# The feed-forward down projection of a hybrid decoder trunk: where its row sums are split, who adds the fourth product's weights, and where the normalisation is emitted

## The chip, the cores and the metric

The kernel runs on one core of one Trainium2 chip. The metric is the device time of one launch in microseconds, the median of several runs; lower is better. The profile comes from one more execution on the same kind of chip, recorded by the hardware profiler. Engines are named as in the profile: PE is TensorE's matmul stream and PEld its weight loads, DVE is VectorE, ACT is ScalarE, POOL is GpSimd, SP is SyncE, which issues transfers.

## The reference

Two layers of a decoder trunk on 512 tokens of 1024 features in float32. Each layer has a feed-forward block, a mixer (a gated linear recurrence and a sliding-window attention side by side), and a second feed-forward block. The change touches the feed-forward blocks, of which the program has four:

```python
def rms_norm(x, gain):
    y = x * rsqrt(mean(x * x, axis=-1, keepdims=True) + EPS)
    return y * gain

def swiglu(h, w_gate, w_up, w_down):          # w_down: 2816 x 1024
    return (silu(h @ w_gate) * (h @ w_up)) @ w_down

for l in range(2):
    x = x + 0.5 * rms_norm(swiglu(rms_norm(x, g0), ...), g1)      # feed-forward 1
    x = x + rms_norm(mixed(rms_norm(x, g2)) @ w_out, g3)          # mixer
    x = x + 0.5 * rms_norm(swiglu(rms_norm(x, g4), ...), g5)      # feed-forward 2
```

## The kernel before, in words

**Precision.** Every float32 product is made of three matmuls in a reduced format: each operand is split into a high part (`hi`, a rounding copy made by ScalarE) and a low part (`lo`, what the copy left over). `lo` is made in one of two ways. `split` lets VectorE subtract (line 426 for activations, line 293 for weights of the quarter products, line 356 for other weights). `split_dma` lets ScalarE write the negated source and GpSimd issue an accumulating transfer that adds the copy's source to it (lines 435 to 437). `mm3` then issues hi x hi, hi x lo and lo x hi.

**The stage.** `down` (line 685) multiplies the activations (22 tiles of 128 features, `src`) by the weights of the down projection. Tokens come in four tiles `t` of 128, outputs in two halves `h` of 512, so there are eight accumulators `y[t][h]`. The features 16 to 21 are multiplied directly (`both`, `piece`): three weight blocks for `h` = 0 first, three for `h` = 1 at the end. The features 0 to 15 go through a Strassen-like scheme of seven products on quarters (`quarters`, line 878): features in two halves, tokens in two halves, outputs in two halves. Each product is 4 weight blocks ("quarters" `q` = 0 to 3 below), each used for 2 feature tiles x 2 token tiles x 3 matmuls of 512 columns, 48 matmuls in all. The order is p1, p3, p7, p2, p6, p5, then the second output half of token tiles 0 and 1, then p4, then the second output half of token tiles 2 and 3.

**Operands.** `Late` makes the left operands: `x1` for p1, `x37` for p3 and p7, `x56` from the row sums `s` for p5 and p6 (`more(k)`, by `split_dma`), `x2[0]` and `x2[1]` from the raw tiles for p2 and p4 (`second`, by `split_dma`). `Stream.quarter` (line 254) makes the right operands, one block per call: raw blocks `u` (for p1 and p7) and `v` (for p2) are loaded by SyncE into four buffers, and sums of quarters live in `b22` (p3, p5) and `b12` (p7, p6, p4). When a raw block is no longer needed, `leave` frees its buffer and issues the next load. A block is split up to four blocks ahead of the one in use; six pairs of `hi` and `lo` exist.

**What is emitted beside the products.** The functions `side1` to `side5` are called at each quarter `q` of their product, and emit work for other engines: row sums, splits, loads, and `fetch`, which loads the gain row and the eight pieces of the residual `x_d` (line 724). `ready(n)` splits the activations 16 to `n`-1 for the second output half.

**The end of the stage.** `half(t, h)` adds the pieces of a result, squares and sums it (line 624) and multiplies it by the gain. `post(t)` finishes the norm and adds the residual (line 831). Then `norm(t)` computes the next sub-layer's pre-norm (line 842), or, in the last feed-forward block of the program, `leave(t)` transposes and stores the output. `pre.turn(0, ...)` transposes token tiles 0 and 1 into the next stage's input after the last matmul of token tile 2, and `pre.turn(1, ...)` does tiles 2 and 3 a little later (line 124 for the transposes).

**What sets the order.** TensorE's instructions keep the order in which the program emits them; a modelled clock (`order.t`) decides where side work such as the transposes is interleaved. For the other engines a scheduler orders instructions by their place in the program and by when it thinks that their inputs are there; instructions given to `pin` keep the program's order among themselves. Engines execute their queues in order, so an instruction that waits holds up all that follow it in its queue.

Of the kernel before, what the change touches and what calls it, by code (L numbers as in the profile page):

```python
# [44 lines left out]
def trunk(ctx: ExitStack, tc: tile.TileContext, xin, wall, gains, lbT, hgain, sinks, c_dist, c_mask, c_ident, out):  # L45
# [109 lines left out]
    class Stream:  # L155
# [98 lines left out]
        def quarter(self, it):  # L254
# [3 lines left out]
            def sums(o, x, y, op):  # L258
                for c in range(2):
                    pin(nc.vector.tensor_tensor(o[c], x[c], y[c], op=op))  # L260

            def raw(i):
                self.load(i + 1)
                return [self.raw[i][:, c] for c in h]

            def leave(i):
                self.raw.pop(i)
                self.freed += 1
                self.load(self.freed + W32)
# [18 lines left out]
            if it.kind == "p7" and q + 1 < it.n:  # L288
                sums(self.b12[q + 1], self.b12[q + 1], self.b22[q + 1], ALU.add)
            elif it.kind == "p6":  # L290
                sums(self.b22[q], self.b22[q], w, ALU.add)
            for c in range(2):
                pin(nc.vector.tensor_tensor(it.lo[:, h[c]], w[c], it.hi[:, h[c]].bitcast(F32), op=ALU.subtract))  # L293
            if it.kind == "p7":

                sums(w, raw(u + q), w, ALU.subtract)
                leave(u + q)
            elif it.kind == "p6":
                for o, x in zip(w, raw(v + q)):
                    nc.gpsimd.dma_start(o, x, accum_op=ALU.add)  # L300
                leave(v + q)
            elif it.kind == "p5":
                self.b22[q] = None
            elif it.kind == "p4":
                self.b12[q] = None
# [379 lines left out]
    def down(src, kt, l, n, nxt, fast):  # L685
# [12 lines left out]
        def ready(n):  # L698

            for i in range(2 * js[0], min(n, kt)):  # L700
                if not isinstance(src[i], tuple):
                    src[i] = split(src[i])
# [31 lines left out]
        if fast:  # L734
# [32 lines left out]
            def side7(q):  # L767
                for k in (2 * q, 2 * q + 1):
                    late.second(0, k)

            def side2(q):
                for k in (2 * q, 2 * q + 1):
                    late.more(k)

            def side6(q):
                for k in (2 * q, 2 * q + 1):
                    late.second(1, k)

            def side5(q):
                if q == 1:  # L780
                    fetch()
                elif q > 1:
                    ready(2 * js[0] + 3 * q - 3)

            more, product = quarters(late, y, (side1, side3, side7, side2, side6, side5))
        else:
# [48 lines left out]
        def norm(t):  # L835
# [5 lines left out]
            for h in range(2):  # L841
                nc.vector.tensor_scalar(pre.xn[t][h], xt[t][h], rc, None, op0=ALU.mult)

        def rest():
            yield WAIT["normed"]
            pre.turn(1, lambda kp: acc() if kp == 0 else aux())
# [4 lines left out]
        bs = [ws.next(8, TT) for _ in last]  # L851
        for t in range(TT):
            if fast and t == 2:
                product(4, [y[t][0] for t in (2, 3)], False)
                for t in (2, 3):
                    half(t, 0)
                t = 2
            for j, b in zip(last, bs):
                for i in range(2):
                    piece(b, t, 1, j, i)  # L860
                    order.poll()
                ws.used(b)
                if pre and (t, j) == ((2, last[-1]) if fast else (3, last[TURN])):
                    pre.turn(0, lambda kp: acc() if kp < 3 else aux())
                    if not fast:
                        norm(2)
            post(t)
            if not pre:
                order.spawn(leave(t))
            elif fast or t != 2:  # L870
                norm(t)
        if pre:
            order.spawn(rest())
        else:
# [696 lines left out]
```

## Time and profile before

| | |
|---|---|
| time, three runs | 2159.26, 2160.92, 2160.66 us, median 2160.66 us |
| the profiled execution: own time, span | 2160.11 us, 2158.3 us |
| mean granted TensorE clock | 0.988 |
| PE busy | 2096.1 us (97%) |
| DVE busy | 1632.0 us (76%) |
| ACT busy | 1243.8 us (58%) |
| POOL busy | 285.1 us (13%) |
| transfers from and to memory | 213.43 MB read, 14.73 MB written |

The span runs from the first to the last instruction; the own time also counts what lies around them. Busy PE does not mean a PE at its peak: the ends of matmuls are modelled, so their start times tell more than their durations. In a group's row the columns are the line, the engine and operation, output and input names, count, busy time and mean duration, and the idle time in front with what ended it. In a row of windows the columns are the stretch, its length, the busy time and count of PE, PEld, DVE, ACT and POOL, the granted clock, the mean busy share of the sixteen DMA engines, and GB/s; an instruction that straddles an edge is counted in both windows. In a timeline a bracket gives the idle time in front of the instruction and what ended it.

### The profile page before, as it was taken

To read this page: it belongs to the slowest core of one execution; us is meant where nothing else is said; L and a number is where in the kernel's file an instruction comes from. 1 tells how busy PE (TensorE), PEld (TensorE's weight loads), DVE (VectorE), ACT (ScalarE), POOL (GpSimd) and SP (SyncE) were. 2 spreads that over 40 slices of the span, in tenths; PEclk is the share of its full clock that TensorE was granted. 3 is DMA by queue.
4 is the path that set the end of the run, shared out by engine and by line. 5 is a ranking of instruction groups with operands and counts; after the bars stand their busy time and mean duration, and the time that the engine had idled before them with its cause. 6 is when DMAs were issued, how large, how long until landed. Compare 5 with 4: busy or idle time off the path is not lost.

```text
span 2158.3 us, 36578 instructions
## 1 busy us (share of the span) xinstructions
PE 2096.1 (97%) x13561; PEld 1871.9 (87%) x13561; DVE 1632.0 (76%) x2889; ACT 1243.8 (58%) x2194; POOL 285.1 (13%) x338
## 2 busy tenths in 40 slices
PE   9999988999999999999899999889999999999987
PEld 8899966877888999997699998678778989999976
DVE  5887877766786778788688778677677758887876
ACT  6565675546454566568455666654553545565673
POOL 0011140000000011114001111400000000111150
PEclk9999999999999999999999999999999999999999
DMA  8677795321246377779638777943121553777793
GB/s 244 156 189 179 190 194 174 108 69 66 72 103 200 98 176 187 184 178 202 182 106 192 182 182 196 200 146 102 59 79 59 132 189 97 188 187 181 194 196 99
DMA packets 169683, 330.18 MB, mean 153 GB/s; under 512 B 19392, under 2 KB 85408, under 8 KB 169504
## 3 DMA queue, kind: packets, MB, share of 16 engines
q1 hardware_dynamic: 122416, 228.16, 31.7%
q0 software_dynamic: 46944, 99.64, 27.5%
q8 instruction: 106, 1.74, 0.3%
q14 instruction: 73, 0.60, 0.1%
q10 hardware_dynamic: 144, 0.05, 0.0%
HBM read 213.43 MB, written 14.73 MB: 106 GB/s over the span
## 4 chain that ended last, share of the span: by engine, by line
PE 83%; DMA 6%; issue 5%; DVE 2%; ACT 2%; POOL 1%; SPq 0%; POOLq 0%; DVEq 0%; ACTq 0%
PE acc L114 61%; PE aux L114 21%; DMA w<-wall 2%; DMA s<-w 2%; PE aux L124 1%; DMA s<-s 1%; DVE wlo L293 1%; PE acc L124 1%; ACT whi L285 1%; DMA s<-wall 0%; SPq L240 0%; DVE s L260 0%; DMA s<-xin 0%; ACT s L624 0%; POOL s L300 0%
## 5 line engine op out<-in xcount | busy, mean ns | idle before, releaser
L114 PE MATMUL acc<-s,whi 128*128 128x256 f32 (+1 forms) x4976 | 1051.7, 309 | 0.4 <-DVE s L426 0.3
L114 PEld LDWEIGHTS acc<-s,whi 128*128 128x128 f32 x4976 | 808.9, 191 | 47.6 <-issue 3.2
L114 PE MATMUL acc<-s,wlo 128*128 128x256 f32 (+1 forms) x2488 | 764.9, 307 | 1.2 <-DMA wlo<-w 1.1
L114 PEld LDWEIGHTS acc<-s,wlo 128*128 128x128 f32 x2488 | 475.2, 191 | 24.2 <-DMA wlo<-w 1.3
L114 PE MATMUL acc<-whi,s 128*128 128x512 f32 x1360 | 454.4, 403 | 27.7 <-DMA s<-s 27.6
L349 ACT CAST whi<-w 128x1024 fp32r<-128x1024 f32 (+1 forms) x309 | 287.0, 932 | 216.6 <-PE acc L114 98.9
L114 PEld LDWEIGHTS acc<-whi,s 128*128 128x128 f32 x1360 | 260.6, 193 | 94.3 <-DMA s<-s 36.0
L349 ACT CAST whi<-tt 128x1024 fp32r<-128x1024 f32 x160 | 167.7, 1048 | 256.8 <-DVE tt L343 197.1
L354 POOL DMA_DIRECT2D wlo<-w x166 | 143.0, 862 | 1203.4 <-DVE wlo L356 495.5
L356 DVE TENSOR_TENSOR wlo<-tt,whi 128x1024 fp32r<-128x1024 f32 x160 | 196.0, 1225 | 138.2 <-ACT whi L349 135.8
L114 PE MATMUL acc<-wlo,s 128*128 128x512 f32 x680 | 271.3, 399 | 18.5 <-DVE wlo L293 18.5
L114 PE MATMUL aux<-s,whi 128*128 128x256 f32 (+1 forms) x1296 | 239.2, 285 | 0.0
L356 DVE TENSOR_TENSOR wlo<-w,whi 128x1024 fp32r<-128x1024 f32 (+1 forms) x143 | 171.9, 1213 | 88.1 <-ACT whi L349 86.5
L114 PEld LDWEIGHTS aux<-s,whi 128*128 128x128 f32 x1296 | 202.7, 192 | 1.1 <-issue 0.5
L114 PE MATMUL aux<-s,wlo 128*128 128x256 f32 (+1 forms) x648 | 184.3, 284 | 0.0
L114 PEld LDWEIGHTS acc<-wlo,s 128*128 128x128 f32 x680 | 131.1, 193 | 46.0 <-DVE wlo L293 19.7
L437 POOL DMA_DIRECT2D s<-s x128 | 124.8, 1159 | 237.0 <-ACT s L425 100.5
L114 PE MATMUL aux<-whi,s 128*128 128x512 f32 x432 | 149.1, 401 | 1.1 <-ACT s L425 1.0
L353 ACT ACTIVATE wlo<-w 128x1024 fp32r<-128x1024 f32 (+1 forms) x166 | 140.7, 847 | 0.0
L293 DVE TENSOR_TENSOR wlo<-s,whi 128x512 fp32r<-128x512 f32 x160 | 102.7, 685 | 30.1 <-ACT whi L285 29.8
L114 PEld LDWEIGHTS aux<-s,wlo 128*128 128x128 f32 x648 | 124.4, 192 | 0.4
L114 PEld LDWEIGHTS aux<-whi,s 128*128 128x128 f32 x432 | 82.5, 192 | 24.7 <-DVE s L426 5.0
(182 smaller groups left out, 2497.5 us busy)
## 6 DMA issues: line engine op xcount, KB each, us to landing
w<-wall SPq DMA_DIRECT2D x267, 512.0 KB, 3.9
wlo<-w POOLq DMA_DIRECT2D x86, 512.0 KB, 5.3
w<-wall SPq DMA_DIRECT2D x224, 128.0 KB, 3.8
wlo<-w POOLq DMA_DIRECT2D x80, 256.0 KB, 3.6
s<-wall SPq DMA_DIRECT2D x128, 128.0 KB, 3.9
s<-s POOLq DMA_DIRECT2D x64, 256.0 KB, 5.3
x_d<-s SPq DMA_DIRECT2D x48, 256.0 KB, 2.0
s<-x_d SPq DMA_DIRECT2D x48, 256.0 KB, 6.4
```

The costliest lines, as they stand in the source:

```text
L114: nc.tensor.matmul(o, lhsT, rhs, start=start, stop=stop)
L124: nc.tensor.transpose(o, src, ident)
L285: i = nc.scalar.copy(it.hi[:, h[c]], w[c])
L293: pin(nc.vector.tensor_tensor(it.lo[:, h[c]], w[c], it.hi[:, h[c]].bitcast(F32), op=ALU.subtract))
L349: i = nc.scalar.copy(it.hi[:, c], w[:, c])
L353: self.hold(nc.scalar.mul(it.lo[:, c], w[:, c], -1.0))
L354: nc.gpsimd.dma_start(it.lo[:, c].bitcast(F32), w[:, c], accum_op=ALU.add)
L356: self.hold(nc.vector.tensor_tensor(it.lo[:, c], w[:, c], it.hi[:, c].bitcast(F32), op=ALU.subtract))
L437: nc.gpsimd.dma_start(lo.bitcast(F32), src, accum_op=ALU.add)
```

## The change

Four edits, all in the feed-forward down projection.

1. The row sums `x56` are split from the third quarter of p7 on: `more(0)` to `more(3)` beside p7, `more(4)` to `more(7)` beside the first two quarters of p2. Before, all eight were beside p2, two per quarter.
2. The weights of p4 (`b12` + `v`) are added by VectorE when p5's block is split, between ScalarE's copy and VectorE's subtraction for p5. Before, GpSimd added them by accumulating transfers when p6's block was split. The raw block `v` is freed at the new place.
3. The splits of the activations 16 to 21 (`ready`) come at p6's last quarter and p5's first, and `fetch` at p5's first quarter. Before, `fetch` was at p5's second quarter and the splits at its third and fourth.
4. `post(0)` stays after the second half of token tile 0; `norm(0)` (or `leave(0)`) and `post(1)` are emitted at p4's second quarter and `norm(1)` (or `leave(1)`) at its third. Before, all of them were emitted ahead of p4.

```diff
@@ Stream.quarter
             elif it.kind == "p6":
                 sums(self.b22[q], self.b22[q], w, ALU.add)
+            elif it.kind == "p5":
+                sums(self.b12[q], raw(v + q), self.b12[q], ALU.add)
+                leave(v + q)
             for c in range(2):
                 pin(nc.vector.tensor_tensor(it.lo[:, h[c]], w[c], it.hi[:, h[c]].bitcast(F32), op=ALU.subtract))
             if it.kind == "p7":
                 sums(w, raw(u + q), w, ALU.subtract)
                 leave(u + q)
-            elif it.kind == "p6":
-                for o, x in zip(w, raw(v + q)):
-                    nc.gpsimd.dma_start(o, x, accum_op=ALU.add)
-                leave(v + q)
             elif it.kind == "p5":
                 self.b22[q] = None
@@ down
             def side7(q):
                 for k in (2 * q, 2 * q + 1):
                     late.second(0, k)
+                    if q > 1:
+                        late.more(k - 4)
             def side2(q):
-                for k in (2 * q, 2 * q + 1):
-                    late.more(k)
+                if q < 2:
+                    for k in (2 * q, 2 * q + 1):
+                        late.more(k + 4)
             def side6(q):
                 for k in (2 * q, 2 * q + 1):
                     late.second(1, k)
+                if q == 3:
+                    ready(2 * js[0] + 3)
             def side5(q):
-                if q == 1:
+                if q == 0:
+                    ready(kt)
                     fetch()
-                elif q > 1:
-                    ready(2 * js[0] + 3 * q - 3)
...
+        def after(t):
+            if not pre:
+                order.spawn(leave(t))
+            elif fast or t != 2:
+                norm(t)
+
+        def side4(q):
+            if q == 1:
+                after(0)
+                post(1)
+            elif q == 2:
+                after(1)
...
             if fast and t == 2:
-                product(4, [y[t][0] for t in (2, 3)], False)
+                product(4, [y[t][0] for t in (2, 3)], False, side=side4)
...
-            post(t)
-            if not pre:
-                order.spawn(leave(t))
-            elif fast or t != 2:
-                norm(t)
+            if not fast or t > 1:
+                post(t)
+                after(t)
+            elif t == 0:
+                post(0)
```

## The prediction

> **What bounds the kernel now.** I read the chain of work that ended last, then the waits, then the stages of the down projection as windows, then the timelines of the places where TensorE waits.
>
> ```profile
> PE 83%; DMA 6%; issue 5%; DVE 2%; ACT 2%; POOL 1%; SPq 0%; POOLq 0%; DVEq 0%; ACTq 0%
> ```
>
> TensorE is the bound, so an edit is worth what it takes out of TensorE's waiting. The waits of TensorE on line 114 inside the feed-forward down projections are two kinds:
>
> ```profile
> PE acc L114 <- DMA s<-s: 27.6, 13, 3.6
> ...
> PE acc L114 <- DVE wlo L293: 18.5, 3, 6.2
> ```
>
> (us in all, times, longest.) The idle time is not the whole loss, because the clock falls behind a wait:
>
> ```profile
> 312.71 0.73 PE L114 MATMUL acc<-whi,s 128*128 128x512 f32 x2 [3.51 <-DMA s<-s]
> ...
> 358.52 0.79 PE L114 MATMUL acc<-wlo,s 128*128 128x512 f32 x1 [6.16 <-DVE wlo L293]
> 359.11 0.63 PE L114 MATMUL acc<-whi,s 128*128 128x512 f32 x1
> 359.54 0.63 PE L114 MATMUL aux<-whi,s 128*128 128x512 f32 x1
> ```
>
> Behind the 6.16 us the matmuls start 0.43 us apart. I therefore cost the stage by difference. The undisturbed rate stands in the chain, 48 matmuls of 512 columns in 10.88 us, 0.2267 us each; eight transposes take 0.87 us:
>
> ```profile
> 257.83 10.88 PE acc L114 x48
> ...
> 2134.01 0.87 PE acc L124 x8
> ```
>
> The four down projections, from the first matmul to the first transposition of the next input (in the last one to the end of its matmuls):
>
> ```profile
> 241.32:366.88 125.56, 111.47 (x464) 87.70 (x463) 97.09 (x177) 80.23 (x169) 34.88 (x40) 0.96 0.78 190
> 950.27:1075.56 125.29, 112.50 (x465) 90.25 (x464) 96.72 (x177) 80.28 (x169) 34.87 (x40) 0.95 0.77 188
> 1311.08:1438.02 126.94, 112.69 (x464) 89.67 (x463) 96.98 (x177) 80.15 (x169) 34.86 (x40) 0.95 0.76 185
> 2021.42:2149.03 127.61, 117.36 (x498) 94.37 (x497) 95.10 (x174) 76.54 (x161) 34.86 (x40) 0.96 0.69 158
> ```
>
> The code issues 72 (first half) + 288 (six products) + 36 + 48 (fourth product) + 18 = 462 matmuls in each of the first three (the rows count two more at the edges), 104.7 us at the undisturbed rate. The last has 480 and two groups of eight transposes, 108.8 + 1.7 = 110.6 us. So 20.8 + 20.6 + 22.2 + 17.0 = 80.6 us are lost in these stages. Where, in the first (columns: PE, PEld, DVE, ACT, POOL busy, clock, DMA share, GB/s):
>
> ```profile
> 301.17:322.20 21.03, 13.78 (x49) 9.31 (x48) 9.65 (x16) 15.00 (x35) 14.21 (x17) 0.92 1.11 209
> 322.20:333.10 10.90, 10.90 (x49) 9.00 (x48) 7.72 (x11) 4.59 (x6) 2.07 (x3) 1.00 1.16 261
> 333.10:343.98 10.88, 10.20 (x38) 6.53 (x38) 9.09 (x15) 6.57 (x15) 0.00 (x0) 1.00 0.76 293
> 343.98:362.77 18.79, 12.63 (x48) 9.97 (x48) 13.34 (x28) 8.11 (x20) 0.00 (x0) 0.82 0.24 89
> ```
>
> These are the sixth product, the fifth, the second output half of token tiles 0 and 1 (36 matmuls, 8.16 us), and the fourth product. They lose 10.15, 0, 2.7 and 7.9 us. Ahead of 301.17 nothing is lost: 241.32 + 264 x 0.2267 is 301.17.
>
> **The change part by part.** *Weights of the fourth product.* Removed are the accumulating transfers of line 300:
>
> ```profile
> L300 POOL DMA_DIRECT2D s<-w x32 | 41.9, 1799 | 6.6 <-DVE wlo L293 4.3 <-DMA s<-w 2.4
> ```
>
> ```profile
> q0 software_dynamic: 2295, 3.99, 92.5%
> ```
>
> The second row is GpSimd's DMA queue from 300 to 325 us (packets, MB, share of the engines): 3.99 MB in 25 us fill the engines to 92.5%, so one transfer of 256 KB costs about 1.6 us. Eight per projection are 13 us of transfer time, queued in front of the row sums for which the sixth product waits. That exceeds the 10.15 us lost, so the queue explains the loss, and without the eight the wait goes. Added are 32 VectorE additions; the nearest row is the same shape with the same operands:
>
> ```profile
> L260 DVE TENSOR_TENSOR s<-w,s 128x512 f32<-128x512 f32 x32 | 20.6, 684 | 0.0
> ```
>
> Eight per projection are 5.5 us on VectorE, between ScalarE's copy of the fifth product's weights and their subtraction. Behind them in VectorE's queue stand that subtraction, the splits of the last six activations and of the last weights. Is there cover? One more row gives the stretch before:
>
> ```profile
> 279.40:301.17 21.77, 21.77 (x97) 18.02 (x96) 20.39 (x34) 16.81 (x36) 9.67 (x14) 1.00 0.77 170
> ```
>
> From 279.40 to 343.98 VectorE is busy 20.39 + 9.65 + 7.72 + 9.09 = 46.9 us. With 5.5 more that is 52.4 us, against 4 x 10.88 + 8.16 = 51.7 us of undisturbed TensorE time. VectorE is at its limit there; what saves it is that the last row holds subtractions for the fourth product, which are not due yet. I take 1 us per projection as lost to it, between ends of 0 and 5.5.
>
> *Raw weights held longer.* The second four raw blocks are now freed by these additions, about one product later in the program, and the loads of the last three weight blocks follow. Before, those loads waited for the slow transfers anyway:
>
> ```profile
> 323.90 1.06 ACT L349 CAST whi<-w 128x1024 fp32r<-128x1024 f32 x1 [5.78 <-DMA w<-wall]
> ...
> 329.55 1.05 ACT L349 CAST whi<-w 128x1024 fp32r<-128x1024 f32 x1 [4.60 <-DMA w<-wall]
> ```
>
> VectorE frees them with less to wait for, so I count nothing against it.
>
> *Row sums split from the seventh product on.* Eight splits per projection (two ScalarE passes and one accumulating transfer each, 8 x 1.6 = 13 us) move into the seventh and early second product. ScalarE has room there, since it stands waiting for weights; the second row is VectorE's last subtraction for the second product:
>
> ```profile
> 290.82 2.06 ACT L285 CAST whi<-w 128x512 fp32r<-128x512 f32 x3 [2.22 <-DMA w<-wall]
> ```
>
> ```profile
> 294.12 0.68 DVE L293 TENSOR_TENSOR wlo<-w,whi 128x512 fp32r<-128x512 f32 x1
> ```
>
> That operand ends at 294.8 and is due when the second product's last quarter starts, at 241.32 + 252 x 0.2267 = 298.4 us: 3.6 us of slack. What crowding does to a weight load shows in the landing times from 276 to 300 and from 300 to 325 us:
>
> ```profile
> w<-wall SPq DMA_DIRECT2D x16, 128.0 KB, 3.9
> ```
>
> ```profile
> w<-wall SPq DMA_DIRECT2D x12, 128.0 KB, 8.7
> ```
>
> 4.8 us later against 3.6 us of slack costs 1.2 us per projection; ends 0 and 4.8. The Trainium skill (DMA: Bandwidth & Descriptors, Queues, rings and completion order) says that an engine takes the queues with work in turn, a packet from each; two busy queues would then at most double a load. An estimate by that page is 3.9 us later and 0.3 us lost, some 3.6 us less over the four; no run here separates it from the 8.7, which is more than double, and I keep the row.
>
> *Splits of the last activations and fetches earlier.* The 2.7 us in front of the fourth product are waits for these splits and a VectorE that works them off late. With the sixth product's transfers gone they come a product earlier; I count this as recovered, less the 1 us above.
>
> *Normalisation in the fourth product.* The fourth quarter's operand is ready to be subtracted long before it is:
>
> ```profile
> 347.46 0.61 ACT L285 CAST whi<-s 128x512 fp32r<-128x512 f32 x1
> ```
>
> ```profile
> 356.38 0.88 DVE L842 TENSOR_SCALAR s<-s,rt 128x512 f32<-128x512 f32 x2
> 357.18 1.29 DVE L293 TENSOR_TENSOR wlo<-s,whi 128x512 fp32r<-128x512 f32 x2
> ```
>
> Its copy ends at 348.1, and VectorE takes it at 357.2, behind the whole chain of both normalisations, which were emitted ahead. After the change the chain is emitted behind it, so the 6.16 us and their slow clock go. What is late next is the transposition of tiles 0 and 1: the chain ended at 357.3, 13.3 us after the fourth product's start, and the transposition is due 10.88 + 4.08 = 15.0 us after it. Moved back one quarter (2.72 us) it is 1.0 us late; two quarters give 3.7, and an unhindered start gives 0. I take 1.0 in each of four.
>
> The sum: 80.6 recovered, less 4 x (1.0 + 1.2 + 1.0) = 12.8, is 67.8 us. The profiled execution took 2160.1 us around its span of 2158.3, as much as the median of 2160.7 to 0.03%: 2160.1 - 67.8 = 2092.3, so 2092 us.
>
> **The rivals.** *VectorE becomes the bound* (for: 52.4 against 51.7 us; against: the fourth product's subtractions can wait): 4.5 us more per projection, 2092 + 18 = 2110 us. *The transfers crowd the second product instead* (for: 8.7 us landings; against: transfers have less than a full share, 0.77, until 301.17): 3.6 us more each, and with the clock behind it some 4, 2108 us. *The normalisation does not really move*, since VectorE's order is chosen by the scheduler and not by the line of emission alone (against: the row at 357.18 follows the emission exactly): 3 x 7.9 = 23.7 us stay, 2116 us. *Slower: the fetch blocks SyncE's queue.* It now comes at the fifth product's start and needs buffers:
>
> ```profile
> 325.13 4.75 SPq L724 DMA_DIRECT2D s<-x_d  x7
> 331.82 0.33 SPq L243 DMA_DIRECT2D w<-wall  x1
> 333.21 0.32 SPq L724 DMA_DIRECT2D s<-x_d  x1
> ```
>
> If the three weight blocks of the second half stood behind it, and it behind the fifth product's operands (free when that product ends, when the half is due), then 8.4 us of issue, 8.7 of landing, 1.1 + 1.2 of splitting and, for the third block, twice the 5.65 us between the copies at 323.90 and 329.55, less 2.7 that run meanwhile, make 28 us, with the slow clock 29. It decides above 20.2 us per projection, the average loss now; here +9 in each, 2160 + 36 = 2196 us. Against it: these loads are issued with the fifth product's splits, four quarters ahead, in front of the fetch.
>
> **How the numbers follow.** Forecast 0.60, VectorE bound 0.16, crowding 0.10, no move 0.08, blocked queue 0.06. Nothing lost at all would give 2160.1 - 80.6 = 2079.5, with the small waits at the transposition of tiles 2 and 3 (0.43 us in the row below) also gone 2078. The range runs from there to 2116, which takes in all but the last case. A measurement of this kernel tells 0.2%, 4.3 us, from no change: faster 0.93, within it 0.01, slower 0.06.
>
> ```profile
> 382.06 0.55 PE L124 MATMUL acc<-ident,s 128*128 128x128 f32 x3 [0.43 <-DVE s L842]
> ```
>
> **What would show it.** Right: no group of line 300 on POOL; the sixth product's window near 10.9 us; the wait of line 114 for s<-s below 5 us in all; no 6 us wait for the fourth product's subtraction; 0.2267 us between matmuls from the first half to the transposition; the four windows near 108 us (112 in the last). Wrong: the wait of line 114 for VectorE grows in the fifth product or the half after it, weight loads are late in the second product, or tiles 0 and 1 are late for their transposition by more than 2 us.

## The result: 2106.5 us, and the profile after

The changed kernel took 2106.48 us (median of five runs, 2102.45 to 2108.89) beside 2159.26 us of the kernel before on the same chip (five runs, 2158.18 to 2160.92). The ratio is 0.9752, with a 95% interval of 0.9738 to 0.9767. The profiled execution took 2106.48 us around a span of 2104.7 us, so the two profiled executions differ by 53.6 us, where 67.8 had been forecast.

The chain of work that ended last still runs over TensorE, with less behind DMA and GpSimd than before:

```profile
PE 78%; DVE 3%; ACT 3%; DMA 1%; issue 1%; SPq 0%; DVEq 0%; ACTq 0%
```

TensorE's waits after (us in all, times, longest):

```profile
PE acc L114 <- DVE wlo L296: 14.3, 4, 5.0
PE acc L124 <- DVE s L845: 5.1, 6, 1.4
```

The wait for `s<-s` (27.6 us before) is gone, and so are the three 6 us waits for the fourth product's weights. The 14.3 us in the first row carry the line number of a quarter's subtraction (293 before, 296 now), but they are other waits. The four stages, in the same windows as in the prediction, from the first matmul to the first transposition (in the last to the end of the matmuls):

```profile
241.17:353.98 112.81, 107.80 (x464) 88.59 (x463) 98.38 (x180) 79.10 (x166) 27.88 (x32) 0.97 0.74 187
938.88:1048.19 109.31, 106.63 (x465) 87.80 (x463) 98.02 (x180) 79.07 (x166) 27.89 (x32) 0.98 0.77 194
1283.94:1395.62 111.68, 107.27 (x464) 88.23 (x463) 98.10 (x180) 78.97 (x166) 27.86 (x32) 0.97 0.75 190
1980.51:2095.30 114.79, 112.56 (x499) 92.73 (x497) 99.32 (x182) 76.06 (x161) 27.85 (x32) 0.99 0.66 158
```

Against 104.73 us undisturbed (110.55 in the last) they lose 8.1 + 4.6 + 7.0 + 4.2 = 23.9 us, where they lost 80.6. The transposition of tiles 2 and 3, behind these windows, waits 1.36 us instead of 0.43 in three of them, 2.8 us more: 80.6 - 23.9 - 2.8 = 53.9, beside the 53.6 us between the two profiled executions. Where the rest is lost, in the first projection (sixth product; fifth; second half of tiles 0 and 1; fourth):

```profile
301.02:311.90 10.88, 10.88 (x49) 9.01 (x48) 10.65 (x19) 10.88 (x28) 4.35 (x8) 1.00 0.63 106
311.90:330.30 18.40, 13.39 (x49) 10.55 (x48) 15.25 (x24) 11.89 (x21) 4.73 (x6) 0.84 0.74 173
330.30:338.50 8.20, 8.20 (x35) 6.72 (x34) 7.29 (x12) 3.10 (x8) 0.00 (x0) 0.94 0.98 370
338.50:349.40 10.90, 10.90 (x49) 9.03 (x49) 9.37 (x20) 5.89 (x13) 0.00 (x0) 1.00 0.31 114
```

The sixth and the fourth product run undisturbed. The border between the last two windows lies two matmuls early: by their first matmuls the half starts at 330.33 and the fourth product at 339.02 us, so the half takes 8.69 us, 0.53 more than its 8.16, at a clock of 0.94. The fifth product, which lost nothing before, takes 18.4 us instead of 10.9. Its timeline on TensorE:

```profile
319.85 0.61 PE L114 MATMUL acc<-whi,s 128*128 128x512 f32 x2
325.47 0.79 PE L114 MATMUL acc<-wlo,s 128*128 128x512 f32 x1 [5.01 <-DVE wlo L296]
326.06 1.05 PE L114 MATMUL acc<-whi,s 128*128 128x512 f32 x2
```

It has the fourth block's `hi` and waits for its `lo`. VectorE's timeline tells why (L425 subtracts for an activation of the second output half, here number 18, L260 adds the fourth product's weights, L296 makes `lo`):

```profile
322.32 0.69 DVE L425 TENSOR_TENSOR s<-s,s 128x512 fp32r<-128x512 f32 x1 [3.12 <-ACT s L424]
322.93 1.29 DVE L260 TENSOR_TENSOR s<-w,s 128x512 f32<-128x512 f32 x2
324.13 1.29 DVE L296 TENSOR_TENSOR wlo<-s,whi 128x512 fp32r<-128x512 f32 x2
```

The fourth block's addition and subtraction stand in VectorE's queue behind the split of activation 18, and that waits 3.12 us for ScalarE's copy. ScalarE's timeline (L348 copies a weight block of the second half, L424 an activation):

```profile
316.30 1.05 ACT L348 CAST whi<-w 128x1024 fp32r<-128x1024 f32 x1 [1.90 <-DMA w<-wall]
317.26 0.61 ACT L424 CAST s<-s 128x512 fp32r<-128x512 f32 x1
320.72 1.04 ACT L348 CAST whi<-w 128x1024 fp32r<-128x1024 f32 x1 [2.85 <-DMA w<-wall]
321.67 1.13 ACT L424 CAST s<-s 128x512 fp32r<-128x512 f32 x2
```

The copies of activations 17 and 18 stand behind weight copies that wait for their loads. So a late load, by way of two in-order queues, holds up an operand that has nothing to do with it. Three questions follow: is it the place of these splits, is it VectorE's added work, or is it the late loads, and what made them late?

### The profile page after: what moved, and what is told of

It is laid out like the page before. It is cut to its first block, busy times and chain, and to the rows that moved or that the text cites. A ratio compares the mean times of both kernels' runs of the same rounds, so it can differ in the third digit from the quotient of the medians.

```text
span 2104.7 us, 36506 instructions
## 1 busy us (share of the span) xinstructions
PE 2077.2 (99%) x13561; PEld 1867.3 (89%) x13561; DVE 1646.5 (78%) x2921; ACT 1242.6 (59%) x2194; POOL 257.5 (12%) x306
## 4 chain that ended last, share of the span: by engine, by line
PE 78%; DVE 3%; ACT 3%; DMA 1%; issue 1%; SPq 0%; DVEq 0%; ACTq 0%
PE acc L114 58%; PE aux L114 18%; DMA w<-wall 1%; PE aux L124 1%; ACT whi L285 1%; PE acc L124 1%; DVE s L834 1%; DVE wlo L355 1%; DVE wlo L296 1%; ACT s L435 0%; SPq L240 0%; DVE s L260 0%; ACT s L434 0%; ACT s L623 0%; DVE s L845 0%
## 5 line engine op out<-in xcount | busy, mean ns | idle before, releaser
L114 PE MATMUL acc<-whi,s 128*128 128x512 f32 x1360 | 446.7, 397 | 0.0
L348 ACT CAST whi<-w 128x1024 fp32r<-128x1024 f32 (+1 forms) x309 | 287.0, 932 | 173.0 <-PE acc L114 94.0
L348 ACT CAST whi<-tt 128x1024 fp32r<-128x1024 f32 x160 | 167.6, 1048 | 255.8 <-DVE tt L342 192.5
L114 PE MATMUL acc<-wlo,s 128*128 128x512 f32 x680 | 269.0, 396 | 14.3 <-DVE wlo L296 14.3
L114 PE MATMUL aux<-whi,s 128*128 128x512 f32 x432 | 144.0, 390 | 0.0
L436 POOL DMA_DIRECT2D s<-s x128 | 111.5, 1164 | 225.0 <-ACT s L424 98.5
L296 DVE TENSOR_TENSOR wlo<-s,whi 128x512 fp32r<-128x512 f32 x160 | 102.7, 685 | 9.9 <-ACT whi L285 9.9
L285 ACT CAST whi<-s 128x512 fp32r<-128x512 f32 x160 | 89.6, 617 | 33.0 <-PE aux L114 21.2
```

Of the source, the lines that this page charges most:

```text
L114: nc.tensor.matmul(o, lhsT, rhs, start=start, stop=stop)
L285: i = nc.scalar.copy(it.hi[:, h[c]], w[c])
L348: i = nc.scalar.copy(it.hi[:, c], w[:, c])
L436: nc.gpsimd.dma_start(lo.bitcast(F32), src, accum_op=ALU.add)
```

## The experiments

Each kernel is the changed one (2106.5 us) with the edit shown. The kernel before, run beside them on the same chip each time, took 2158.2 to 2159.8 us; the numbers in brackets are the ratio to it and its 95% interval. The changed kernel was not run beside them, so differences from it are judged by these intervals.

### The last splits behind the fifth product's fourth block (late3), and edit 3 undone (u3)

```
 def side6(q):                                  # late3
     ...
-    if q == 3:
-        ready(2 * js[0] + 3)
```

> The changed kernel with one emission moved: the split of the last three of the fifth product's activations (ready(19)) comes at the fifth product's first quarter, behind the subtraction of that product's fourth weight block, instead of at the sixth product's last quarter, ahead of it. Theory T (VectorE serves its queue in order; the splits of activations 17 and 18 wait for ScalarE copies that stand behind weight copies whose loads are late, and the fourth block's addition and subtraction wait behind them): the four waits of TensorE for that block (5.01, 2.68, 4.41, 2.23 us) go to below 0.5 us each, the fifth product's window in the first projection falls from 18.4 us (with its first group of the half) by some 7 us, and the time to 2085 to 2091 us. Rival R1 (VectorE has too much to do with the 32 added additions): VectorE's work is the same, so the wait only moves to the activations of the half behind; 2100 to 2107 us. Rival R3 (the late loads of the last weights decide): the half behind waits for those weights or for the splits instead; 2097 to 2105 us.

```
 def side6(q):                                  # u3: late3, and
 ...
 def side5(q):
-    if q == 0:
-        ready(kt)
+    if q == 1:
         fetch()
+    elif q > 1:
+        ready(2 * js[0] + 3 * q - 3)
```

> The changed kernel with its third edit alone undone: the last splits of the fifth product's activations in its third and fourth quarter again, and the fetch in its second. T: the splits stand behind the fourth block's subtraction, so the four waits for it (14.3 us with some 7 us of slow clock) go; the splits come later for the half behind, which may wait 1 to 3 us in each projection: 2088 to 2100 us, faster than the changed kernel. The prediction as written (the third edit recovers 2.7 us in each projection): 2117 us. R1: 2105 to 2112 us.

Measured: late3 2112.56 us (0.9791, 0.9778 to 0.9805), u3 2109.15 us (0.9769, 0.9756 to 0.9782). late3 is slower than the changed kernel (0.9738 to 0.9767); u3 is not told apart from it and lies in R1's range, though its waits (14.4 us in all) are for ScalarE's copies of activations and not for VectorE. Theory T, as I had put it, fell, and late3 came out above the ranges of all three expectations. Its first half held: in late3 the fifth product doesn't wait for its fourth block any more. But the wait is only handed on. TensorE's timeline of late3, in the half behind (`aux`):

```profile
325.11 0.50 PE L114 MATMUL aux<-whi,s 128*128 128x512 f32 x1 [1.75 <-ACT s L424]
...
327.75 0.67 PE L114 MATMUL aux<-whi,s 128*128 128x512 f32 x1 [1.41 <-ACT s L424]
...
341.61 0.50 PE L114 MATMUL acc<-wlo,s 128*128 128x512 f32 x1 [1.44 <-DVE wlo L296]
```

Now the activations are late for their own product, behind the same weight copies, and the fourth product's weights after them. Undoing edit 3 (u3) gives a wait of 4.08 us for such an activation. So the place of the splits chooses who waits; it doesn't remove the lateness. That is what R3 had said of the waits, though not of the time. Edit 3 is worth 2.7 us in all, less than the 4.3 us that can be told from nothing.

### VectorE's additions behind the subtraction (behind)

```
 elif it.kind == "p5":
-    sums(self.b12[q], raw(v + q), self.b12[q], ALU.add)
-    leave(v + q)
 for c in range(2):
     pin(nc.vector.tensor_tensor(it.lo[...], w[c], it.hi[...], op=ALU.subtract))
 ...
 elif it.kind == "p5":
+    sums(self.b12[q], raw(v + q), self.b12[q], ALU.add)
+    leave(v + q)
     self.b22[q] = None
```

> The changed kernel with VectorE's eight additions per projection put behind the subtraction of the same weight block instead of ahead of it (each block waits for one addition less; the raw blocks come free one subtraction later). Theory T: the stall is the queue order ahead of both, so the waits for the fourth block shrink only by the addition's 1.29 us each: 4 x 1.29 and some clock, 2098 to 2104 us. R1 (the additions as such): the waits shrink to those that remain without the additions' place in the path, the same 5 us, but VectorE's total is unchanged; no further fall, 2100 to 2106 us. R3 (late loads): the raw blocks are freed later, the last weights' loads come later by 1.4 us each, and the time rises to 2106 to 2112 us.

Measured: 2098.30 us (0.9721, 0.9708 to 0.9735), 8.2 us less than the changed kernel and within T's range. R3's rise did not come. TensorE's waits on line 114:

```profile
PE aux L114 <- DVE wlo L354: 6.4, 8, 1.2
...
PE acc L114 <- DVE wlo L293: 2.7, 3, 1.4
```

14.3 us of waits have become 9.1, spread over eleven, the longest 1.4 us. The value is T's, but not by T's account, so it is in part luck: the waits for the fourth block fell by 11.6 us (14.3 to 2.7), not by 4 x 1.29, and 6.4 us of waits for the second half's weights are new. ScalarE's timeline shows what else changed:

```profile
318.43 1.14 ACT L423 CAST s<-s 128x512 fp32r<-128x512 f32 x2
321.07 1.04 ACT L347 CAST whi<-w 128x1024 fp32r<-128x1024 f32 x1 [1.50 <-DMA w<-wall]
```

The copies of activations 17 and 18 now stand together, ahead of the second weight copy that waits; in the changed kernel that of 18 stood behind it. VectorE's split of activation 18 starts at 320.28 us instead of 322.32. So of the 3.6 us that the first projection's wait lost (5.01 to 1.43), the addition's place accounts for 1.2 and the earlier split for 2.0; the rest is TensorE's own later arrival.

### Each of the first two edits undone (u1, u2), and both (u12)

```
 def side7(q):                                  # u1: edit 1 undone
     ...
-        if q > 1:
-            late.more(k - 4)
 def side2(q):
-    if q < 2:
-        for k in (2 * q, 2 * q + 1):
-            late.more(k + 4)
+    for k in (2 * q, 2 * q + 1):
+        late.more(k)
```

> The changed kernel with the row sums' place alone undone: all eight are split in the second product again, as before. The prediction's step (the eight accumulating transfers of weights, gone here, were what stood ahead of the row sums): without them the row sums come through in time, the sixth product loses nothing or one short wait, 2104 to 2112 us. Rival (each of the two edits alone lifts the wait only in part, since the row sums are 13 us of transfers in a product of 10.9 us): the sixth product waits for the row sums 2 to 5 us in each projection, 2115 to 2135 us.

```
-elif it.kind == "p5":                          # u2: edit 2 undone
-    sums(self.b12[q], raw(v + q), self.b12[q], ALU.add)
-    leave(v + q)
 ...
+elif it.kind == "p6":
+    for o, x in zip(w, raw(v + q)):
+        nc.gpsimd.dma_start(o, x, accum_op=ALU.add)
+    leave(v + q)
```

> The changed kernel with the fourth product's weights added by GpSimd's accumulating transfers again, in place of VectorE's additions (the other three edits kept). The prediction's theory (the eight transfers stand ahead of the row sums): the row sums are split from the seventh product on, so most of them are through before the eight transfers are issued, but those of the second eight are not: the sixth product waits again, 4 x 3 to 5 us, and the time is 2115 to 2130 us. R1 (VectorE's additions make the fifth product's stall): that stall goes, 2085 to 2095 us if the row sums are early enough. T: the order of the splits ahead of the fourth block is unchanged, the stall stays or grows as the buffers of the copies are freed by transfers standing in the same queue: 2115 us or more.

u12 has both of these diffs:

> The changed kernel with both of the first two edits undone: row sums split in the second product and the fourth product's weights added by GpSimd's accumulating transfers, as before; the last splits' place and the normalisation's place stay as changed. It completes the square: with both edits 2106.5, without the row sums' edit 2097.6, without the additions' edit 2112.4. If either edit alone takes the wait in the sixth product away (neither of those two kernels shows it): here it is back, about 6 us per projection with slow clock as before (10.15 us per projection), and the time is 2097.6 + 4 x 10 = 2138 us, 2130 to 2148. If the wait was taken away by the last splits' place instead: the sixth product waits for less than 1 us each and the time is 2100 to 2115 us.

| row sums split | fourth product's weights added by | median us | ratio to before |
|---|---|---|---|
| in the second product | GpSimd's transfers (u12) | 2125.23 | 0.9846 (0.9832 to 0.9859) |
| from the seventh on | GpSimd's transfers (u2) | 2112.44 | 0.9788 (0.9774 to 0.9801) |
| in the second product | VectorE (u1) | 2097.55 | 0.9715 (0.9700 to 0.9729) |
| from the seventh on | VectorE (changed) | 2106.48 | 0.9752 (0.9738 to 0.9767) |

Only u12 waits for row sums; its waits have the row

```profile
PE acc L114 <- DMA s<-s: 26.1, 12, 3.5
```

and neither u1 nor u2 has such a row. So either edit alone clears the sixth product, as the prediction said of the second. With VectorE's additions in place, the first edit costs 8.9 us. What it does can be read off u1 against the changed kernel. The loads of weight blocks from 276 to 300 us, their landing in us, changed kernel and then u1:

```profile
w<-wall SPq DMA_DIRECT2D x16, 128.0 KB, 4.6
```

```profile
w<-wall SPq DMA_DIRECT2D x16, 128.0 KB, 3.6
```

and VectorE's last subtraction for the second product, and its first addition for the fourth, in the changed kernel and in u1:

```profile
297.01 0.69 DVE L296 TENSOR_TENSOR wlo<-w,whi 128x512 fp32r<-128x512 f32 x1 [0.35 <-ACT whi L285]
...
309.36 1.29 DVE L260 TENSOR_TENSOR s<-w,s 128x512 f32<-128x512 f32 x2
```

```profile
293.73 0.68 DVE L296 TENSOR_TENSOR wlo<-w,whi 128x512 fp32r<-128x512 f32 x1
...
306.72 1.28 DVE L260 TENSOR_TENSOR s<-w,s 128x512 f32<-128x512 f32 x2
```

With the row sums' transfers beside them the loads land 1.0 us later, VectorE ends the second product's weights 3.3 us later, and twelve microseconds on it is still 2.6 us behind. The loads are not the whole of it. ScalarE's timeline of the changed kernel, its fourth copy of a raw block in this stretch and its last:

```profile
290.43 0.62 ACT L285 CAST whi<-w 128x512 fp32r<-128x512 f32 x1 [3.63 <-DMA w<-wall]
...
296.36 0.62 ACT L285 CAST whi<-w 128x512 fp32r<-128x512 f32 x1
```

In u1 these two start at 287.85 and 292.91 us. The fourth is 2.6 us later and waits for its load; between it and the last, ScalarE waits for nothing, but eight passes of `split_dma` (L434 and L435) stand among the weight copies, four for the row sums and four for the second product's activations, where u1 has none; the lag grows to 3.45 us. The additions free the raw buffers 2.6 us later, and the last weight blocks' loads start as much later (the first issue at 310.71 us instead of 308.06). On ScalarE the order differs too. In u1:

```profile
315.02 0.62 ACT L424 CAST s<-s 128x512 fp32r<-128x512 f32 x1
315.55 1.05 ACT L348 CAST whi<-w 128x1024 fp32r<-128x1024 f32 x1
316.50 0.62 ACT L424 CAST s<-s 128x512 fp32r<-128x512 f32 x1
318.61 1.05 ACT L348 CAST whi<-w 128x1024 fp32r<-128x1024 f32 x1 [1.50 <-DMA w<-wall]
```

The copies of activations 17 and 18 each stand one weight copy further ahead, and the first weight copy doesn't wait. TensorE then waits 0.32 us for the fifth product's fourth block instead of 5.01:

```profile
320.68 0.50 PE L114 MATMUL acc<-wlo,s 128*128 128x512 f32 x1 [0.32 <-DVE wlo L296]
```

u1 is the fastest version that I ran. None of the three expectations held in full. No expectation had u1 below 2104, though the sixth product waits for nothing there, as the first of them said. u2 lies 3 us below its range, and it waits for other things than I thought: 10.1 us for the fifth product's fourth block and 12.7 us for the second half's weights, nothing in the sixth product. u12 waits in the sixth product as expected, but came out 13 us below its 2138: it is 27.7 us above u1, where I had added 40. The later products of u12 wait for nothing, and tiles 0 and 1 come to their transposition in time, where u1 waits 3 x 2.40 us; that loads and VectorE catch up while TensorE waits would explain it, but no run shows that alone.

### The same stall loosened in two other ways (r2, early2)

r2 emits the last three splits one quarter earlier, so that their copies stand ahead of two of the three weight copies:

```
 def side6(q):
     ...
-    if q == 3:
+    if q == 2:
         ready(2 * js[0] + 3)
```

> The changed kernel with the split of the last three of the fifth product's activations emitted one quarter earlier (the sixth product's third quarter), so that their ScalarE copies stand ahead of two of the three weight copies that wait for loads. If the order in ScalarE's queue (activations' copies behind weight copies that wait for late loads) makes the fifth product's stall: the wait for the fourth block falls from 5.0, 2.7, 4.4, 2.2 us to below 1.5 us each and the half behind doesn't wait: 2086 to 2098 us. If VectorE's load as such makes it: the wait stays or moves to the weights of the half, 2102 to 2110 us. If late loads make it, wherever the copies stand: TensorE waits in the half for the last weights, 2100 to 2108 us.

early2 begins the fourth product's activations, whose eight transfers run together with the last weight blocks' loads, half a product earlier:

```
 def side2(q):
     if q < 2:
         ...
+    else:
+        for k in (2 * q - 4, 2 * q - 3):
+            late.second(1, k)
 def side6(q):
-    for k in (2 * q, 2 * q + 1):
-        late.second(1, k)
+    if q < 2:
+        for k in (2 * q + 4, 2 * q + 5):
+            late.second(1, k)
```

> The changed kernel with the eight splits of the fourth product's activations (two ScalarE passes and one accumulating transfer each) begun half a product earlier: four in the second product's second half, four in the sixth product's first half. In the changed kernel their eight transfers run from 309.5 us on, together with the loads of the last three weight blocks, and the buffers of the last activations' copies come free behind them. If this crowding makes the loads and the copies late: ScalarE's waits for the last weight blocks (1.9, 2.9, 0.7 us in the first projection) shrink by half or more, and the time falls to 2088 to 2099 us. If the loads are late because their raw buffers come free late (behind VectorE's additions): the waits stay, 2103 to 2109 us. If the second product is now crowded instead: it waits for its weights, 2108 to 2120 us.

Measured: r2 2104.82 us (0.9752, 0.9738 to 0.9767), not told apart from the changed kernel; early2 2100.04 us (0.9727, 0.9712 to 0.9741), 6.4 us less, though the two intervals just touch. In early2 ScalarE's waits for those loads fell from 5.5 to 4.0 us in the first projection, less than the half that I expected, and TensorE's for the fourth block, over all four, from 14.3 to 9.5 us. The time lies just above the range of 2088 to 2099. So the crowding is a part at most, since in early2 the loads also start 1.5 us earlier (309.25 us instead of 310.71). In r2 TensorE's waits are

```profile
PE acc L124 <- DVE s L845: 11.3, 6, 2.4
PE acc L114 <- DVE wlo L296: 8.9, 4, 2.9
```

The 8.9 us are not for the fourth block any more. VectorE's split of activation 18 (from 316.95 us, after 1.56 us of waiting for ScalarE) now stands ahead of the third block's addition and subtraction too, and TensorE waits for the third block: 2.56, 2.85, 2.20 and 1.29 us. That is 5.4 us less than before, and 6.2 us more stand at the transpositions: handed on again, to the block ahead and to the normalisation.

### Two remedies together, and the end of the stage (u1b, u1bn, u1t, u4)

u1b joins u1's diff and behind's.

> The changed kernel with the row sums split in the second product again and VectorE's additions put behind the subtraction of the same block. If the two remedies act on the same stall (the fourth block of the fifth product, whose wait is down to 0.3 us in the first projection with the first remedy alone): little is left for the second, 2093 to 2098 us. If they act on separate losses (the first on ScalarE's copies, 8.9 us; the second on VectorE's queue, 8.2 us): 2086 to 2091 us. If the additions' later place makes the last weights' loads late: 2098 to 2104 us.

u1bn is u1b with the normalisation a quarter earlier:

```
 def side4(q):
-    if q == 1:
+    if q == 0:
         after(0)
         post(1)
-    elif q == 2:
+    elif q == 1:
         after(1)
```

> The kernel of the two remedies together (row sums in the second product, additions behind the subtraction) with the normalisation of token tiles 0 and 1 emitted one quarter earlier (the fourth product's first and second quarter). In the run with the row sums' edit undone the transposition of tiles 0 and 1 waits 2.4 us for that chain and the fourth product waits for nothing. If the chain stands late because of its place: the wait falls by up to 2 us in three projections, with the clock behind it 4 to 7 us less than the two remedies alone, 2082 to 2092 us. If VectorE has no room ahead of the fourth product's last subtractions: that product waits instead, and the time is the same within 4 us or higher, 2092 to 2104 us.

u1t is u1 with the transposes later in TensorE's order:

```
-if pre and (t, j) == ((2, last[-1]) if fast else (3, last[TURN])):
+if pre and (t, j) == (3, last[0 if fast else TURN]):
 ...
-    normed=7600.0
+    normed=9000.0
```

> The best version so far (the changed kernel with the row sums split in the second product again, 2097.6 us) with TensorE's two groups of transposes put later: those of tiles 0 and 1 behind six more matmuls (1.36 us), those of tiles 2 and 3 about 1.4 us later among the next stage's matmuls. In that version TensorE waits 3 x 2.40 and 3 x 1.34 us there for VectorE's normalisation. If these waits are only a matter of order (VectorE delivers at the same time, TensorE does other work meanwhile): 3 x 1.36 + 3 x 1.34 = 8 us less, 2088 to 2092 us. If VectorE is the bound of the stretch (it was busy 45.2 of 49.2 us from the sixth product to the transposition): the wait comes back behind the transposes, where VectorE subtracts what they deliver, and the time stays within 4 us, 2094 to 2101 us.

u4 is the changed kernel with edit 4 undone:

```
-product(4, [y[t][0] for t in (2, 3)], False, side=side4)
+product(4, [y[t][0] for t in (2, 3)], False)
 ...
-if not fast or t > 1:
-    post(t)
-    after(t)
-elif t == 0:
-    post(0)
+post(t)
+if not pre:
+    order.spawn(leave(t))
+elif fast or t != 2:
+    norm(t)
```

> The changed kernel with the normalisation of token tiles 0 and 1 emitted again ahead of the fourth product. The prediction's step: the chain stands again ahead of the fourth product's last subtraction in VectorE's queue, so a wait of about 6 us with its slow clock comes back in each of the first three projections, less the 1.36 us that the normalisation in the fourth product costs later: 3 x (7.9 - 1.4) = 19.5 us more, 2122 to 2130 us. Rival (VectorE runs ahead of TensorE behind the fifth product's waits of the changed kernel, so that the chain has cover): 2106 to 2114 us.

Measured: u1b 2103.65 us (0.9747, 0.9733 to 0.9760), u1bn 2121.26 (0.9827, 0.9814 to 0.9840), u1t 2105.55 (0.9750, 0.9736 to 0.9764), u4 2134.47 (0.9888, 0.9872 to 0.9905). Each remedy alone gave over 8 us, the two together 2.8, which is not told from nothing. The value lies in the range of u1b's third expectation, loads made late by the additions' later place, but the timelines show another cause for most of it. TensorE's row in u1b:

```profile
328.10 0.50 PE L114 MATMUL aux<-wlo,s 128*128 128x512 f32 x1 [2.08 <-DVE wlo L354]
```

This is a wait for the second of the half's three weight blocks; u1 has none there, and 0.96 us at the third. VectorE's timeline in u1b, and the same subtraction in u1:

```profile
326.22 0.69 DVE L424 TENSOR_TENSOR s<-s,s 128x512 fp32r<-128x512 f32 x1 [1.92 <-ACT s L423]
326.82 1.22 DVE L354 TENSOR_TENSOR wlo<-w,whi 128x1024 fp32r<-128x1024 f32 x1
```

```profile
321.15 2.35 DVE L355 TENSOR_TENSOR wlo<-w,whi 128x1024 fp32r<-128x1024 f32 x2
```

In u1 VectorE subtracts for the first two blocks in a row. In u1b the second subtraction stands behind the split of an activation for whose copy VectorE waits 1.92 us, although all three weight copies had ended by 323.0 us. The loads do start 2.0 us later than in u1 (310.04 us), but the 2.08 us are the queue's order again.

In u1bn the wait at the transposition (2.40 us in u1's first projection) turns up elsewhere; in u1t it stays (2.88 us) and another comes behind it. A timeline row from each:

```profile
349.86 0.79 PE L114 MATMUL acc<-wlo,s 128*128 128x512 f32 x1 [4.71 <-DVE rt L627]
```

```profile
360.88 0.39 PE L114 MATMUL acc<-s,whi 128*128 128x256 f32 x1 [2.05 <-DVE s L614]
```

In the first VectorE does the normalisation ahead of the fourth product's last subtraction (the profile names the instruction behind that subtraction as what ended the wait; in the third projection it names the subtraction); in the second TensorE comes later to the transposes and then waits for VectorE to subtract what they deliver. These are the mechanisms of the second expectation of each, but both times lie above its range, u1t 8.0 us above u1. In these stages VectorE is close to its limit. From 301 to 350 us, changed kernel and u1:

```profile
301.00:350.00 49.00, 43.99 (x182) 35.80 (x181) 43.19 (x72) 31.79 (x68) 9.11 (x11) 0.93 0.66 180
```

```profile
301.00:350.00 49.00, 45.70 (x200) 36.90 (x198) 44.81 (x77) 35.35 (x76) 10.09 (x12) 1.00 0.80 210
```

43.2 and 44.8 of 49 us (DVE is the third pair). u4 shows the opposite end: with the normalisation ahead of the fourth product again, the old wait returns beside the fifth product's (4.05 us in the first projection), and the time rises by 28.0 us, more than the 15.5 to 23.5 that I expected:

```profile
351.50 0.79 PE L114 MATMUL acc<-wlo,s 128*128 128x512 f32 x1 [6.24 <-DVE wlo L296]
```

## Why the prediction came out as it did

The sign, the bound and the three places where time was to be recovered were right, and 2106.5 us lies within 2078 to 2116. The value of 2092 was 14 us too low. By its steps:

- **The eight transfers and the sixth product.** Right. The sixth product takes 10.88 us, and u1 shows that taking the transfers out of the queue is enough.
- **Crowding of the second product's weight loads, 1.2 us each.** This is the term that was mis-sized, not in its mechanism but in where it is paid. The loads landed 1.0 us later in the median, far from the 4.8 between the two rows that I used, and the second product lost nothing: 241.17 + 264 x 0.2267 is 301.02, where the sixth product begins. The 3.6 us of slack were TensorE's. VectorE had no such slack: it came out of the second product 3.3 us late, and the fifth product's fourth block paid. Nor had ScalarE the room that I gave it: its fourth weight copy there started 2.6 us late behind a late load, and `split_dma`'s passes between the copies added the rest. Undoing this edit takes 8.9 us off, where the term held 4 x 1.2 = 4.8. The Trainium skill (DMA: Bandwidth & Descriptors, Queues, rings and completion order) has a DMA engine serve the queues with work in turn, a packet from each. With one more busy queue and packets of like size a load would by that take up to twice as long; 3.6 to 4.6 us lies within it, and the estimate by it of 0.3 us lost in the second product was nearer than my 1.2. Neither speaks of what the late block does to the queues behind it.
- **VectorE at its limit, 1 us each, ends 0 to 5.5.** The loss did fall on the fifth product, and VectorE's queue is where it is passed on; yet VectorE stood idle for 3.12 us just ahead of the stall, so it wasn't its busy time alone. I had counted 52.4 us of work against 51.7 us and asked whether the sum fits. The question to ask was which instruction in the queue can wait, and for whom. The prediction's list of signs against it held the right one: the wait for VectorE did grow in the fifth product.
- **Raw weights held longer, counted at nothing.** Wrong. The loads that these additions release are the ones for which ScalarE waits 5.5 us in the first projection. How much of that is the additions' doing is not shown: in early2, where the same additions run and the transfers beside the loads are moved, it is 4.0, and the loads start 1.5 us earlier.
- **Earlier splits and fetch, counted as 2.7 us recovered in each.** The half behind the fifth product waits for nothing any more (8.7 us, 0.5 of it slow clock), but the wait was exchanged for the fifth product's. The edit is worth 2.7 us in all four, not in each, and that is not told from nothing. Its place ahead of the fourth block was in the diff, and I didn't ask what was queued behind the splits.
- **Normalisation.** Right, and about to size: 7.9 - 1.0 in each would be 27.6 us in four, and u4 is 28.0 us slower. That agreement is in part luck: u4's waits in the fifth product are also 1.4 us longer. Tiles 0 and 1 were 0.34 us late in three projections, in u1 and r2 2.4, all between the ends of 0 and 3.7; why the one or the other is not shown. A cost that I had left out is the transposition of tiles 2 and 3: it waits 1.36 us, and 0.44 in u4, so the 2.8 us over three projections belong to this edit.
- **The rivals.** The time lies between the forecast and VectorE as the bound (2110). u1bn and u1t show that rival at work in the last part of the stage. The slower one did not come: the fetch is issued from 328.8 us, and TensorE never waits for a weight block behind it.

By removals the edits are worth 18.7 us (the first two together, u12), 2.7 (the third) and 28.0 (the fourth), 49.4 of the 52.8 us gained; they need not add up, since the waits are handed on. The prediction's figures of the first projection, times four, were 4 x (10.15 - 1.0 - 1.2) = 31.8, 10.8 and 27.6 us. The shortfall stands in the first two lines.

Left open: in u1 both the loads' time and ScalarE's order change, and no run moves the loads' time alone. r2 has u1's order of the three weight copies and of activations 16 to 18, with late loads (2.93 us of waiting ahead of the first, none in u1) and one block more behind the splits on VectorE; it gains nothing that can be told from zero. So that order alone was not enough there.

## What to carry to other kernels

When a wait disappears, every engine that had used it to catch up loses that time, so look for the next late operand and not only at the engine that waited: here one TensorE wait was cured twice, and the second cure cost 8.9 us. When work moves to an in-order queue, list what stands directly behind each moved instruction and what it waits for in its turn; an instruction that waits for a load should not stand ahead of one that is due. Put an addition that isn't urgent behind the subtraction that is: 8.2 us here for two moved lines, but look at the other engines' order afterwards: it had changed too, and in the first projection it took more off the wait (2.0 us) than the addition (1.2 us).

## What the runs showed of the hardware

The slow clock behind a wait can come late, and it lasts a while. Behind the 5.01 us wait, 13 matmuls took 5.71 us at a granted clock of 0.50:

```profile
325.47:331.18 5.71, 5.71 (x13) 4.46 (x14) 5.71 (x8) 4.35 (x9) 0.00 (x0) 0.50 0.50 169
```

That is 2.8 us more than their 2.95; 2.4 of it fall into the fifth product and make up, with the wait, its 7.5 us, and the rest into the half behind. In early2 the clock fell only after TensorE had resumed, in TensorE's timeline:

```profile
323.31 0.50 PE L114 MATMUL acc<-wlo,s 128*128 128x512 f32 x1 [2.85 <-DVE wlo L296]
323.65 0.64 PE L114 MATMUL acc<-whi,s 128*128 128x512 f32 x2
324.12 0.53 PE L114 MATMUL acc<-wlo,s 128*128 128x512 f32 x1
324.45 1.05 PE L114 MATMUL acc<-whi,s 128*128 128x512 f32 x2
```

Matmuls start 0.43 us apart from 324.45 us on, four microseconds after the wait began. The Trainium skill (TensorE: Matmul & The Clock Gate, Part 1: The HAM clock gate) says that the clock is halved after an idle window of about 3.4 us. The half rate agrees (0.43 against 0.2267 us); the length doesn't quite, since here a wait of 2.85 us sufficed. Nor is there one length in these runs: in u1b a wait of 2.08 us (328.10 us) was followed by matmuls 0.43 us apart and one of 2.27 us (1023.46 us) by none, and in the changed kernel's last projection they were 0.43 us apart at once behind 2.23 us. Behind waits of 1.43, 1.08 and 0.64 us in a row, in the kernel with the additions behind the subtraction, the granted clock stayed at 1.00:

```profile
322.22 0.50 PE L114 MATMUL acc<-wlo,s 128*128 128x512 f32 x1 [1.43 <-DVE wlo L293]
```

```profile
317.00:333.00 16.00, 12.76 (x52) 9.26 (x51) 13.46 (x20) 11.57 (x20) 0.00 (x0) 1.00 0.77 232
```

So a long wait that is broken into waits of about a microsecond can save more than the waiting itself.
